# Weight sums a group later, a second tile's weights prepared in the mixer, and late value copies on ScalarE

## The chip, the cores and the metric

The kernel runs on one core of a Trainium2 chip, with float32 inputs and one output of 1024 x 1024. The metric is the time of one execution on the device in microseconds (us); of several runs the median counts. Five engines work beside each other, each on its own queue in its own order: TensorE (PE, matrix products into the eight PSUM banks), VectorE (DVE), ScalarE (ACT), GpSimd (POOL) and SyncE (SP). Transfers between the chip's memory and SBUF are issued from SP's and ACT's queues.

## The reference

A decoder block for 1024 tokens of width 1024, in float32. A state-space branch and an attention branch read one normalised input, are gated, added and projected; then come attention into 256 memory tokens and a SwiGLU feed-forward part. Cut to what matters here:

```python
def reference(x, mem, ...):
    u = rms_norm(h, norm_mix[l])
    proj = u @ w_in[l]
    u_ssm, q, k, v, f_logit, gate_logits = jnp.split(proj, [...], axis=-1)
    y_ssm = jax.nn.gelu(s5_ssm(u_ssm, ...))
    glu_a, glu_b = jnp.split(y_ssm @ w_glu[l], 2, axis=-1)
    out_a = glu_a * jax.nn.sigmoid(glu_b)
    att = forgetting_attention(q, k, v, f_logit + b_forget[l])
    out_b = att @ w_fox_o[l]
    gate_a, gate_b = jnp.split(jax.nn.sigmoid(gate_logits), 2, axis=-1)
    h = h + (gate_a * out_a + gate_b * out_b) @ w_mix_out[l]
    h = h + memory_cross_attention(rms_norm(h, norm_mem_q[l]), ...)
    f_a, f_b = jnp.split(rms_norm(h, norm_ffn[l]) @ w_ffn_in[l], 2, axis=-1)
    h = h + (jax.nn.silu(f_a) * f_b) @ w_ffn_out[l]
    return rms_norm(h, norm_final)
```

## The kernel before, in words

**Products.** PE multiplies in a reduced format; each float32 operand is split into a high and a low part, and a product is three matmuls (high by high, high by low, low by high), lines L167 to L169 and L617. The split is the helper `split`: a cast on ACT (L177) and a subtraction on DVE (L178). Weights come through `wload`: a load on SP into `raw` (two buffers, L153), then a split into `whi` and `wlo` (four buffers each). The large products with w_mix_out and the feed-forward weights go by seven products of half size in place of eight; these need sums and differences of blocks of both operands.

**Stages.** stage_in normalises and projects. stage_ssm runs 32 gate products (`gates`, 16 row blocks by two halves) and puts the four groups q of the state space between them (`todo`): `turn_weights` builds the tile Ts and shifts it by three small transfers (L1442), `toeplitz` copies it to Tt on ACT (L1447), `states` loads xg (L1453) and runs the scan, `out` multiplies by Tt (L1503). Beside them go the sums of w_mix_out's blocks that the mixer wants later (`jobs`): `mix_fetch` loads two tiles wk on SP (L491), `mix_sums` does four additions on DVE (L500), `mix_store` stores the four results to sums_d on SP (L504); wk has two buffers. Then comes the attention, and behind it stage_tail.

**The gate loop of stage_tail.** It runs over j from 0 to 7, eight row blocks of 128 channels. For j above 3 `glu.values(j)` loads weights and multiplies; `Glu.value` copies each of the two products (128 x 512) from PSUM to the tile sg, on DVE, at L1186. `glu.rest(j)` multiplies for the sigmoid (ACT, L1191), multiplies sg by it on DVE (L1192), and by the gate ga on POOL (L1199, loads at L1198). Three steps behind, `fox_part(j - 3)` multiplies the attention's output, loads gb (L545), multiplies it by the product in PSUM (L577), adds it to sg (L578), splits (A11, S3 for j below 4; A12, A22, S1, S2 above) and stores to am_d (L585) or s3_d (L593); `minuend` loads am_d back as xm (L563). PSUM banks are shared out as mm 3, sc 2, pv 2, misc 1, so that a product waits until the copy or multiplication of an earlier one has emptied its bank.

**Weights ahead.** The first two of the feed-forward part's weight tiles are prepared early. `ahead(j)` gives five steps: `fetch` loads two tiles wpr of 512 KB on SP (L642); `plain`, `sums`, `seventh` and `rest` split and add (L655 to L660 on DVE) and store seven tiles of 512 KB to w_d from ACT's queue (L633). The feed-forward stage reads w_d back much later.

**The mixer.** For the products n = 1, 2, 6, 5, 3, 7, 4 `mix_weights(n)` loads and splits weights (n = 1, 2, 3 from w_mix_out, the others from sums_d), `mix_mm(n, i)` runs four strips i of twelve matmuls, `mix_add` adds them to the tiles h. After each strip of n = 2, 6, 5 one step of the list `side` runs; it holds the two steps `mix_s4`, which load s3_d and split it. After the strips of n = 3 and n = 4 `scaled` writes the normalised rows to tiles xs, which `turned` transposes on PE.

**What sets the order.** The program is written in this order, and a scheduler then places the instructions of each engine, keeping dependences. `tc.issue_after(ins)` keeps the instructions inside it from being placed ahead of `ins` on ins's own engine. Tiles come from pools: `slot` takes one of 16 buffers, `tmp` one of 5 (shared with sg, xs and others), and a new tile in a buffer waits for the last use of the old one.

Of the kernel before, what the change touches and what calls it, by code (L numbers as in the profile page):

```python
# [9 lines left out]
F32 = mybir.dt.float32  # L10
F32R = mybir.dt.float32r
# [55 lines left out]
def f32(ap):  # L67
    return ap.bitcast(F32)
# [223 lines left out]
def hybrid_block_kernel(ctx: ExitStack, tc: tile.TileContext, x, mem, norm_mix, w_in, b_forget,  # L292
# [36 lines left out]
    with tc.tile_pool(name="st2", bufs=1, reuse_waits="tile") as s2:  # L329
        stage_tail(B, big, s2, sh, x, glu, aT, gate_d, kv_d, sums_d, w_fox_o, w_mix_out, norm_mem_q[0], w_mem_q,  # L330
                   w_mem_o, norm_ffn[0], w_ffn_in, w_ffn_out, norm_final, out)
# [124 lines left out]
def stage_ssm(B, s5, qp, uT, w_in, gate_d, u_d, y_d, w_mix_out, sums_d):  # L456
# [48 lines left out]

    jobs = {}
    for k in range(4):
        for i, f in ((7 * k + 2, mix_fetch), (7 * k + 3, mix_sums), (7 * k + 4, mix_store)):
            jobs[i] = lambda f=f, k=k: f(k)

    mark = []
# [18 lines left out]
def stage_tail(B, big, s2, sh, x, glu, aT, gate_d, kv_d, sums_d, w_fox_o, w_mix_out, g_mq, w_mem_q, w_mem_o, g_ffn,  # L530
# [7 lines left out]
    def slot(dt=F32, name="t"):  # L538
        return s2.tile([P, D], dt, tag="t", bufs=NS2, name=name)

    tmp = sh.tmp
# [16 lines left out]
    def give(name, mk, k, src):  # L558
        B.split(*[a[k // 2][:, k % 2, :] for a in operand(name, mk)], src)

    def minuend(j):
        xm[j] = s2.tile([P, D], F32, tag=("gbc", "xs")[j % 2], bufs=1, name="xm")
        S.dma_start(xm[j], am_d[j - 4])  # L563
# [63 lines left out]
    w_d = B.dram.tile([AHEAD_IN, 7, P, D], F32, name="w_d")  # L627
    pre = {}

    def ahead(j):  # L630

        def keep(n, t_):
            A.dma_start(w_d[j, n], f32(t_))  # L633

        def pair(n):
            hl = slot(F32R, "wph"), slot(F32R, "wpl")
            return hl, [[t_[:, o:o + 512] for t_ in hl] for o in (0, 512)]

        def fetch():
            pre[j] = [slot(name="wpr") for _ in range(2)]  # L640
            for r_, c in zip(pre[j], (0, FH)):
                S.dma_start(r_.rearrange("p (k c) -> p k c", k=8),  # L642
                            w_ffn_in[:, c + j * P:c + (j + 1) * P].rearrange("(k p) c -> p k c", p=P))

        def plain():
            hl, _ = pair(0)
            B.split(*hl, pre[j][0])
            for i, t_ in enumerate(hl):
                keep(i, t_)

        def sums():
            ra, rb = pre[j]
            b22 = rb[:, 512:]
            hl, (w5, w6) = pair(2)
            V.tensor_add(ra[:, 512:], ra[:, 512:], b22)  # L655
            V.tensor_add(ra[:, :512], ra[:, :512], rb[:, :512])
            V.tensor_add(rb[:, :512], rb[:, :512], b22)
            B.split(*w5, ra[:, :512])
            V.tensor_add(ra[:, 512:], ra[:, 512:], ra[:, :512])
            V.tensor_add(ra[:, :512], ra[:, :512], b22)  # L660
            B.split(*w6, ra[:, :512])
            for i, t_ in enumerate(hl):
                keep(2 + i, t_)

        def seventh():
            e_ = slot(F32R, "wph")
            B.split(e_[:, :512], e_[:, 512:], pre[j][1][:, :512])
            keep(4, e_)

        def rest():  # L670
            ra, rb = pre.pop(j)
            hl, (w3, w4) = pair(5)
            B.split(*w3, rb[:, 512:])
            B.split(*w4, ra[:, 512:])
            for i, t_ in enumerate(hl):
                keep(5 + i, t_)

        return [fetch, plain, sums, seventh, rest]

    ahead0, ahead1 = ahead(0), ahead(1)  # L680
    for j in range(8):
        if j > 3:
            for f in glu.values(j):
                f()
        glu.rest(j)
        with B.tc.issue_after(glu.mark.ins):
            for f in {0: ahead0[:1], 1: ahead0[1:2], 2: ahead0[2:3], 3: ahead0[3:] + ahead1[:1], 4: ahead1[1:2],
                      5: ahead1[2:3], 6: ahead1[3:]}.get(j, []):
                f()
        if j == 6:  # L690
            minuend(4)
            minuend(5)
        if j > 2:
            fox_part(j - 3)
# [30 lines left out]
    def mix_s4(kk):  # L725
        y = s2.tile([P, D], F32, tag=("xs", "gbc")[kk], bufs=1, name="s4")
        S.dma_start(y, s3_d[kk])
        for k in range(2):
            give("S4", slot, 2 * kk + k, y[:, 512 * k:512 * k + 512])

    side = [lambda kk=kk: mix_s4(kk) for kk in range(2)]
    mix_weights(6)
    for i in range(4):
        mix_add(1, i)
# [166 lines left out]
    def w_fetch(j):  # L901
        raws[j] = B.wpool.tile([P, RAW], F32, tag="raw", bufs=2, name="raw")[:, :D], tmp("rawb")
        for r_, c in zip(raws[j], (0, FH)):
            f = S.dma_start(r_.rearrange("p (k c) -> p k c", k=8),
                            w_ffn_in[:, c + j * P:c + (j + 1) * P].rearrange("(k p) c -> p k c", p=P))
        return f
# [156 lines left out]
    for j in range(2, NF):  # L1063
# [7 lines left out]
        f = w_fetch(j + 2) if j + 2 < NF else f  # L1071
# [91 lines left out]
class Glu:  # L1163
# [19 lines left out]

    def value(self, j, h):
        ps, dst = self.product(j, h, 0)
        self.B.V.tensor_copy(dst, ps)  # L1186

    def sigmoid(self, j, h):
        ps, dst = self.product(j, h, 1)
# [20 lines left out]
class S5:  # L1210
# [146 lines left out]
    def slot(self, name, bufs=1):  # L1357
        return self.qp.tile([P, D], F32, tag=name, bufs=bufs, name=name)
# [551 lines left out]
```

## Time and profile before

| | |
|---|---|
| median of 3 runs | 1607.4 us (1603.07 to 1611.19) |
| profiled execution, its own time | 1597.43 us |
| its span | 1595.6 us |
| mean granted clock of PE | 0.984 |
| instructions | 20523 |
| moved by transfers | 258.69 MB, mean 162 GB/s |

The profile is one execution, recorded by the hardware. A row of the timeline gives start and length in us, engine, line, operation, output and inputs, and in brackets the idle time of the engine just before and what ended it. A row of the waits gives engine and line, what it waited for, the total in us, how many times, and the longest. A row of the windows gives for a stretch of time the length, then the busy time of PE, its weight loads, DVE, ACT and POOL with the number of instructions, then PE's granted clock, the busy share of the transfer engines and GB/s. A row of the chain gives start, length, engine, tile and line.

### The profile page before, as it was taken

To read this page: it belongs to the slowest core of one execution; us is meant where nothing else is said; L and a number is where in the kernel's file an instruction comes from. 1 tells how busy PE (TensorE), PEld (TensorE's weight loads), DVE (VectorE), ACT (ScalarE), POOL (GpSimd) and SP (SyncE) were. 2 spreads that over 40 slices of the span, in tenths; PEclk is the share of its full clock that TensorE was granted. 3 is DMA by queue.
4 is the path that set the end of the run, shared out by engine and by line. 5 is a ranking of instruction groups with operands and counts; after the bars stand their busy time and mean duration, and the time that the engine had idled before them with its cause. 6 is when DMAs were issued, how large, how long until landed. Compare 5 with 4: busy or idle time off the path is not lost.

```text
span 1595.6 us, 20523 instructions
## 1 busy us (share of the span) xinstructions
PE 1527.3 (96%) x7301; PEld 1257.5 (79%) x7301; DVE 1067.9 (67%) x1900; ACT 669.6 (42%) x1191; POOL 247.9 (16%) x323
## 2 busy tenths in 40 slices
PE   5799899999999899999999989999999999999997
PEld 5688788898777668778788778888888888788886
DVE  5757666435687776888665687777677776565455
ACT  5422343422566553333345564333333333344342
POOL 3015434110121123320101200010000000000001
PEclk8999999999999999999999999999999999999999
DMA  8747745552032635977322177445444544796642
GB/s 272 143 95 170 232 122 113 126 177 31 1 68 44 163 101 180 318 244 259 120 89 84 53 272 251 156 159 165 165 152 153 164 161 147 269 389 221 193 156 106
DMA packets 202869, 258.69 MB, mean 162 GB/s; under 512 B 36024, under 2 KB 127064, under 8 KB 202256
## 3 DMA queue, kind: packets, MB, share of 16 engines
q1 hardware_dynamic: 196144, 241.67, 50.5%
q10 hardware_dynamic: 6624, 15.73, 2.6%
q8 instruction: 57, 0.93, 0.2%
q14 instruction: 44, 0.36, 0.1%
HBM read 176.08 MB, written 83.20 MB: 162 GB/s over the span
## 4 chain that ended last, share of the span: by engine, by line
PE 75%; DVE 8%; DMA 8%; issue 3%; ACT 3%; POOL 2%; SPq 1%; DVEq 0%; POOLq 0%; ACTq 0%
PE mm L967 14%; PE pv L967 7%; PE mm L167 6%; PE mm L169 6%; PE mm L168 6%; PE mm L1104 4%; PE sc L967 4%; PE sc L1104 3%; PE pv L1104 3%; PE sc L167 2%; PE sc L169 2%; PE sc L168 2%; PE mm L617 2%; PE misc L1104 1%; DMA Ts<-Ts 1%
## 5 line engine op out<-in xcount | busy, mean ns | idle before, releaser
L178 DVE TENSOR_TENSOR wlo<-raw,whi 128x1024 fp32r<-128x1024 f32 (+2 forms) x126 | 133.4, 1061 | 114.0 <-ACT whi L177 113.4
L177 ACT CAST whi<-raw 128x1024 fp32r<-128x1024 f32 (+2 forms) x127 | 115.6, 913 | 133.8 <-PE mm L168 38.0
L167 PE MATMUL mm<-uh,whi 128*128 128x512 f32 x344 | 138.2, 402 | 2.4 <-ACT whi L177 2.3
L178 DVE TENSOR_TENSOR ol<-or,oh 128x1024 fp32r<-128x1024 f32 x73 | 89.3, 1224 | 70.8 <-ACT oh L177 69.7
L169 PE MATMUL mm<-uh,wlo 128*128 128x512 f32 x344 | 135.7, 395 | 0.0
L168 PE MATMUL mm<-ul,whi 128*128 128x512 f32 x344 | 135.4, 394 | 0.0
L177 ACT CAST oh<-or 128x1024 fp32r<-128x1024 f32 x73 | 76.8, 1052 | 103.7 <-PE mm L1104 35.3
L999 POOL TENSOR_TENSOR g<-a,c 128x512 f32<-128x512 f32 x22 | 35.6, 1619 | 394.7 <-ACT a L998 374.8
L196 POOL TENSOR_TENSOR r<-ms,mhalf 128x1 f32<-128x1 f32 (+1 forms) x30 | 19.9, 666 | 372.9 <-DVE ms L192 345.3
L1729 POOL TENSOR_TENSOR pl<-pf,ph 128x512 fp32r<-128x512 f32 (+1 forms) x32 | 39.5, 1235 | 244.0 <-DVE ph L1728 198.4
L167 PEld LDWEIGHTS mm<-uh,whi 128*128 128x128 f32 x344 | 65.5, 190 | 14.7 <-ACT whi L177 2.7
L169 PEld LDWEIGHTS mm<-uh,wlo 128*128 128x128 f32 x344 | 65.3, 190 | 14.7 <-DVE wlo L178 1.3
L168 PEld LDWEIGHTS mm<-ul,whi 128*128 128x128 f32 x344 | 65.4, 190 | 11.0
L1726 ACT ACTIVATE pf<-sc 128x512 f32<-128x512 f32 (+1 forms) x96 | 46.4, 490 | 49.1 <-DVE sc L1722 29.4
L967 PE MATMUL pv<-S3h,we 128*128 128x512 f32 x176 | 58.1, 389 | 0.0
L1199 POOL TENSOR_TENSOR sg<-sg,ga 128x512 f32<-128x512 f32 x16 | 36.8, 2318 | 72.6 <-DVE sg L1192 50.8
L167 PE MATMUL mm<-yh,whi 128*128 128x512 f32 x104 | 41.8, 402 | 2.4 <-DVE sg L1186 2.4
L1732 DVE TENSOR_TENSOR pl<-pf,ph 128x512 fp32r<-128x512 f32 (+2 forms) x64 | 35.6, 558 | 10.1 <-ACT ph L1731 9.4
L169 PE MATMUL mm<-yh,wlo 128*128 128x512 f32 x104 | 41.6, 400 | 0.0
L168 PE MATMUL mm<-yl,whi 128*128 128x512 f32 x104 | 41.4, 398 | 0.0
L1104 PE MATMUL mm<-oh 128*128 128x512 f32 x106 | 41.2, 389 | 0.0
L1104 PE MATMUL mm<-ol,oh 128*128 128x512 f32 x106 | 41.2, 389 | 0.0
(680 smaller groups left out, 4581.8 us busy)
## 6 DMA issues: line engine op xcount, KB each, us to landing
or<-c_d SPq DMA_DIRECT2D x77, 256.0 KB
wo<-in_w_ffn_out_dram SPq DMA_DIRECT2D x22, 512.0 KB
c_d<-g SPq DMA_DIRECT2D x44, 256.0 KB
t_d<-wo SPq DMA_DIRECT2D x44, 256.0 KB
or<-t_d SPq DMA_DIRECT2D x44, 256.0 KB
raw<-in_w_ffn_in_dram SPq DMA_DIRECT2D x20, 512.0 KB
rawb<-in_w_ffn_in_dram SPq DMA_DIRECT2D x20, 512.0 KB
raw<-in_w_in_dram SPq DMA_DIRECT2D x18, 512.0 KB
```

The lines of the kernel that those rows point to most:

```text
L167: T.matmul(ps, lh, rh, start=first, stop=False)
L168: T.matmul(ps, lh, rl, start=False, stop=False)
L169: T.matmul(ps, ll, rh, start=False, stop=last)
L177: self.A.copy(hi, src)
L178: (self.G if pool_lo else self.V).tensor_sub(lo, src, f32(hi))
L967: T.matmul(ps, l_[:, k, :], r_, start=first and k == 0 and i == 0, stop=k == 3 and i == 2, skip_group_check=True)
L999: G.tensor_mul(g[:, 512:], a1, c1)
L1104: T.matmul(ps, l_[:, gi], r_[:, 512:], start=n < 3 and p == 0 and k == 0 or n == 7 and p == 0 and k == 0, stop=p == NP - 1 and k == 2, ski ...
L1199: self.B.G.tensor_mul(self.out[j][:, cs], self.out[j][:, cs], ga)
L1726: self.exp = A.activation(pf[:, off:], ps[:, off:], AF.Exp)
L1729: G.tensor_sub(pl[:, off:], pf[:, off:], f32(ph[:, off:]))
L1732: V.tensor_sub(pl[:, off:], pf[:, off:], f32(ph[:, off:]))
```

## The change

Three parts. The jobs on w_mix_out's sums get the places 9 to 11, 16 to 18, 23 to 25 and 29 to 31 in the list of gate products; they had 2 to 4, 9 to 11, 16 to 18 and 23 to 25. The five steps of `ahead(1)` leave the gate loop (they stood at j = 3 to 6) and join `side`, between the strips of the mixer's products, with tiles from `tmp`; `ahead(0)` now has one step at each j from 0 to 4. And `Glu.value` copies on ACT for j above 3.

```diff
@@ -505,7 +505,7 @@
 
     jobs = {}
     for k in range(4):
-        for i, f in ((7 * k + 2, mix_fetch), (7 * k + 3, mix_sums), (7 * k + 4, mix_store)):
+        for i, f in enumerate((mix_fetch, mix_sums, mix_store), (9, 16, 23, 29)[k]):
             jobs[i] = lambda f=f, k=k: f(k)
 
     mark = []
...
@@ -627,17 +627,17 @@
     w_d = B.dram.tile([AHEAD_IN, 7, P, D], F32, name="w_d")
     pre = {}
 
-    def ahead(j):
+    def ahead(j, mk):
 
         def keep(n, t_):
             A.dma_start(w_d[j, n], f32(t_))
 
         def pair(n):
-            hl = slot(F32R, "wph"), slot(F32R, "wpl")
+            hl = mk("wph", F32R), mk("wpl", F32R)
             return hl, [[t_[:, o:o + 512] for t_ in hl] for o in (0, 512)]
 
         def fetch():
-            pre[j] = [slot(name="wpr") for _ in range(2)]
+            pre[j] = [mk("wpr") for _ in range(2)]
             for r_, c in zip(pre[j], (0, FH)):
                 S.dma_start(r_.rearrange("p (k c) -> p k c", k=8),
                             w_ffn_in[:, c + j * P:c + (j + 1) * P].rearrange("(k p) c -> p k c", p=P))
...
@@ -663,7 +663,7 @@
                 keep(2 + i, t_)
 
         def seventh():
-            e_ = slot(F32R, "wph")
+            e_ = mk("wph", F32R)
             B.split(e_[:, :512], e_[:, 512:], pre[j][1][:, :512])
             keep(4, e_)
...
@@ -677,16 +677,15 @@
 
         return [fetch, plain, sums, seventh, rest]
 
-    ahead0, ahead1 = ahead(0), ahead(1)
+    ahead0, ahead1 = ahead(0, lambda name, dt=F32: slot(dt, name)), ahead(1, tmp)
     for j in range(8):
         if j > 3:
             for f in glu.values(j):
                 f()
         glu.rest(j)
         with B.tc.issue_after(glu.mark.ins):
-            for f in {0: ahead0[:1], 1: ahead0[1:2], 2: ahead0[2:3], 3: ahead0[3:] + ahead1[:1], 4: ahead1[1:2],
-                      5: ahead1[2:3], 6: ahead1[3:]}.get(j, []):
-                f()
+            if j < 5:
+                ahead0[j]()
         if j == 6:
             minuend(4)
             minuend(5)
...
@@ -728,7 +727,8 @@
         for k in range(2):
             give("S4", slot, 2 * kk + k, y[:, 512 * k:512 * k + 512])
 
-    side = [lambda kk=kk: mix_s4(kk) for kk in range(2)]
+    side = [ahead1[0]] + [lambda kk=kk: mix_s4(kk) for kk in range(2)] + ahead1[1:2] + [lambda: None] + ahead1[2:3] + \
+        [lambda: None] + ahead1[3:]
     mix_weights(6)
     for i in range(4):
         mix_add(1, i)
...
@@ -1183,7 +1183,10 @@
 
     def value(self, j, h):
         ps, dst = self.product(j, h, 0)
-        self.B.V.tensor_copy(dst, ps)
+        if j < 4:
+            self.B.V.tensor_copy(dst, ps)
+        else:
+            self.B.A.copy(dst, ps)
 
     def sigmoid(self, j, h):
         ps, dst = self.product(j, h, 1)
```

In the changed kernel the lines from L1187 on are three lower in the file: L1191, L1192 and L1198 are L1194, L1195 and L1201, L1442 and L1453 are L1445 and L1456; the copy on ACT is L1189.

**Sums of the state groups, on SP.** Before, SP's queue where the first group's xg load (L1453) stands; wk are the tiles of the sums, raw the gate products' weights:

```order
L491 DMA wk_1317<-in_w_mix_out_dram 128x1024
L491 DMA wk_1318<-in_w_mix_out_dram 128x1024
L1453 DMA xg_1425<-u_d_77 128x1024
L504 DMA sums_d_84<-wk_1317 128x512 x2
L504 DMA sums_d_84<-wk_1318 128x512
L491 DMA wk_1757<-in_w_mix_out_dram 128x1024
L504 DMA sums_d_84<-wk_1318 128x512
L504 DMA sums_d_84<-wk_1757 128x512
L491 DMA wk_1758<-in_w_mix_out_dram 128x1024
L153 DMA raw_1659<-in_w_in_dram 128x4x256
```

The change, at the same place:

```order
L1456 DMA xg_1413<-u_d_77 128x1024
L491 DMA wk_1745<-in_w_mix_out_dram 128x1024
L491 DMA wk_1746<-in_w_mix_out_dram 128x1024
L504 DMA sums_d_84<-wk_1745 128x512 x2
L504 DMA sums_d_84<-wk_1746 128x512 x2
L491 DMA wk_2185<-in_w_mix_out_dram 128x1024
L491 DMA wk_2186<-in_w_mix_out_dram 128x1024
L153 DMA raw_1647<-in_w_in_dram 128x4x256
L504 DMA sums_d_84<-wk_2185 128x512
L153 DMA raw_1653<-in_w_in_dram 128x4x256
```

xg has moved ahead of the first two wk, the four stores of the first group stand together, and both wk of the second group stand ahead of the two raw loads.

**The value copies.** Before, DVE's queue from the second tile's split (wpl) to the first value copy of j = 5 (L1186, sg_6419):

```order
L178 TENSOR_TENSOR S3l_6274<-sg_5719,S3h_6272 128x512
L178 TENSOR_TENSOR wlo_6536<-raw_6532,whi_6535 128x1024
L178 TENSOR_TENSOR wpl_6354<-wpr_6221,wph_6353 128x1024
L577 TENSOR_TENSOR gb_6372<-gb_6372,pv_6359 128x512
L578 TENSOR_TENSOR sg_5802<-sg_5802,gb_6372 128x512
L577 TENSOR_TENSOR gb_6389<-gb_6389,pv_6376 128x512
L178 TENSOR_TENSOR A11l_6267<-sg_5802,A11h_6265 128x512
L578 TENSOR_TENSOR sg_5802<-sg_5802,gb_6389 128x512
L1186 COPY sg_6419<-mm_6406 128x4x128
```

The change, on ACT's queue, with the two copies of j = 5 (L1189, sg_6409); whi_6630 is the weight cast of j = 7, wph and wpl here are the first tile's:

```order
L1194 ACTIVATE sb_6332<-sc_6319 128x512
L177 CAST whi_6512<-raw_6509 128x1024
L633 DMA w_d_6033<-wpl_6342 128x1024
L177 CAST whi_6630<-raw_6627 128x1024
L1189 COPY sg_6409<-mm_6396 128x4x128
L177 CAST A11h_6253<-sg_5802 128x512
L1189 COPY sg_6409<-mm_6411 128x4x128
L177 CAST S3h_6260<-sg_5802 128x512
```

The copies have left DVE and stand on ACT behind a weight cast and a store of the first tile, one on each side of A11h.

**SP ahead of fox_part(4).** Before, SP's queue from the gb loads of fox_part(3) to those of fox_part(4), with what each row waits for:

```order
L545 DMA gb_6652<-gate_d_79 128x512 [waits DMAHW2_49,DVE_49]
L153 DMA raw_6958<-in_w_mix_out_dram 128x2x512 [waits DMAHW4_49,DVE_49]
L585 DMA am_d_6031<-sg_5972 128x1024 [waits DMAHW6_49,DVE_49]
L153 DMA raw_6964<-in_w_mix_out_dram 128x2x512 [waits DMAHW7_49,DVE_49]
L1198 DMA ga_6730<-gate_d_79 128x512 [waits DMAHW0_49,Pool_49]
L1198 DMA ga_6733<-gate_d_79 128x512 [waits DMAHW1_49]
L545 DMA gb_6755<-gate_d_79 128x512 [waits DMAHW2_49]
L545 DMA gb_6778<-gate_d_79 128x512 [waits DMAHW3_49,DVE_49]
```

The change, at the same place:

```order
L153 DMA raw_6923<-in_w_mix_out_dram 128x2x512 [waits DMAHW4_49,DVE_49]
L153 DMA raw_6929<-in_w_mix_out_dram 128x2x512 [waits DMAHW6_49,DMAHW5_49,DVE_49]
L585 DMA am_d_6031<-sg_5972 128x1024 [waits DVE_49]
L642 DMA wpr_7058<-in_w_ffn_in_dram 128x8x128 [waits DMAHW7_49,DMAHW6_49,DVE_49]
L1201 DMA ga_6695<-gate_d_79 128x512 [waits DMAHW1_49,DMAHW0_49,Pool_49]
L1201 DMA ga_6698<-gate_d_79 128x512
L545 DMA gb_6720<-gate_d_79 128x512 [waits DMAHW2_49]
L545 DMA gb_6743<-gate_d_79 128x512 [waits DMAHW3_49,DVE_49]
```

The raw load that stood behind the am_d store now stands ahead of it, and behind the store stands the first half of the second tile's fetch (wpr_7058, L642), ahead of the ga and gb loads.

## The prediction

> **What bounds the kernel now.** I read the page first, then the TensorE waits, then the rows around the waits that lie in the two stages the change touches.
>
> ```profile
> PE 1527.3 (96%) x7301; PEld 1257.5 (79%) x7301; DVE 1067.9 (67%) x1900; ACT 669.6 (42%) x1191; POOL 247.9 (16%) x323
> ```
>
> TensorE (PE) is busy 96% of the span and the change adds or removes no matmul. So it can only give or take idle time of PE, and time in which PE runs at a lower clock. The waits of PE in the two stages:
>
> ```profile
> PE pv L1503 <- ACT Tt L1447: 3.6, 1, 3.6
> PE pv L167 <- DVE gb L577: 2.8, 1, 2.8
> PE mm L167 <- DVE sg L1186: 2.4, 1, 2.4
> PE pv L1460 <- DMA xg<-u_d: 1.6, 1, 1.6
> PE misc L222 <- DVE u2l L178: 1.3, 1, 1.3
> ```
>
> The first and fourth lie in the state groups (stage_ssm, 168 and 196 us), the second and third in the gate loop of stage_tail (713 and 667 us), the fifth in the mixer (796 us). Together 11.7 us, 0.7% of the run: that is the ceiling, apart from the clock.
>
> **First stall of the tail, 667 us.** The rows of PE, then the granted clock (PEclk, third number from the right) of three windows, each behind a stall:
>
> ```profile
> 666.78 0.39 PE L168 MATMUL mm<-yl,whi 128*128 128x512 f32 x1
> 667.00 0.39 PE L169 MATMUL mm<-yh,wlo 128*128 128x512 f32 x1
> 669.84 0.50 PE L167 MATMUL mm<-yh,whi 128*128 128x512 f32 x1 [2.45 <-DVE sg L1186]
> ...
> 674.28 0.40 PE L167 MATMUL pv<-ath,whi 128*128 128x512 f32 x1
> ...
> 690.64 0.39 PE L167 MATMUL pv<-ath,whi 128*128 128x512 f32 x1
> ...
> 715.85 0.50 PE L167 MATMUL pv<-ath,whi 128*128 128x512 f32 x1 [2.84 <-DVE gb L577]
> ```
>
> ```profile
> 670.30:673.80 3.50, 3.50 (x10) 2.71 (x9) 1.36 (x3) 2.06 (x3) 0.00 (x0) 0.51 0.73 277
> 712.50:716.00 3.50, 0.66 (x4) 0.24 (x3) 1.41 (x3) 0.00 (x0) 2.16 (x2) 1.00 0.88 328
> 172.00:175.40 3.40, 3.29 (x15) 3.29 (x16) 0.00 (x0) 0.66 (x2) 2.77 (x13) 0.50 0.20 77
> ```
>
> Matmuls start 0.22 to 0.23 us apart when nothing holds them (666.78, 667.00), so the one at 669.84 is 669.84 - 667.00 - 0.23 = 2.6 us late. Behind it the clock is halved: 12 matmuls take 674.28 - 669.84 = 4.44 us in place of 12 x 0.227 = 2.7, another 1.7 us. This place costs **4.3 us**. What it waits for is a copy on VectorE (DVE), L1186:
>
> ```profile
> 662.66 1.21 DVE L178 TENSOR_TENSOR wpl<-wpr,wph 128x1024 fp32r<-128x1024 f32 x1
> ...
> 664.80 0.69 DVE L577 TENSOR_TENSOR gb<-gb,pv 128x512 f32<-128x512 f32 x1 [0.94 <-DMA gb<-gate_d]
> ...
> 668.72 1.07 DVE L1186 COPY sg<-mm 128x512 f32<-128x512 f32 x1
> ```
>
> The copy of value(5, 0) stands in program order behind the second tile's split (wpl) and a gb that waits for its load, and so its mm bank comes free at 669.8. In the changed kernel it is on ScalarE (ACT), behind one weight cast. ACT at this time is nearly empty:
>
> ```profile
> 666.85 0.62 ACT L177 CAST A11h<-sg 128x512 fp32r<-128x512 f32 x1 [6.45 <-DVE sg L578]
> ...
> 672.84 0.59 ACT L1191 ACTIVATE sb<-mm 128x512 f32<-128x512 f32 x1
> ```
>
> An ACT pass over a 128x512 PSUM bank takes 0.59 us (L1191). The bound below is nothing, the bound above 1.07 (the DVE copy); I take 0.6. The cast ahead (whi_6630) needs its raw weights: before, their load stood on SP behind a wpr fetch, am_d, ga, gb and xm; now it stands ahead of all but the gb of group 0, so some 8 us earlier. The last thing ACT waits for ahead of the copy is the first tile's wpl split on DVE, at about 660 by adding up the DVE rows between. So the copy runs at about 662.5 to 663.5, against 667.2 when PE needs it: 4 us of margin. I take the whole 4.3 as gained. If the raw load were as slow as before (it takes 8 us then) the margin is gone, and up to 2 us of stall stay.
>
> By the Trainium skill, "TensorE: Matmul & The Clock Gate", section "Why this matters for your kernels", the clock falls only after idle gaps of more than about 3 us; by it this stall would not have halved the clock, and the sum below would be 1.7 us smaller. The rows here go against it in both directions: 2.45 us of idle is followed by a clock of 0.51, 2.84 us at 713 by 1.00; the measured rows decide.
>
> **Second stall of the tail, 713 us.** The chain of work that ended last runs through SP's queue:
>
> ```profile
> 707.12 1.14 DVE wlo L178
> 708.27 0.38 SPq L153
> ...
> 709.74 5.28 DMA gb<-gate_d
> 715.11 0.70 DVE gb L577
> ```
>
> The gb of fox_part(4) is issued only at 709.74, because SP stood ahead of it at the am_d store and a raw load, both waiting for DVE; it lands 5.28 us later, frees a pv bank, and fox_part(5) starts at 715.85, 2.84 us after PE was idle, 3.0 after it could have started. DVE is late because of what the change takes off it in this stretch (640 to 720 us, by groups):
>
> ```profile
> L1186 DVE COPY sg<-mm 128x512 f32<-128x512 f32 x8 | 8.9, 1133 | 0.0
> L178 DVE TENSOR_TENSOR wpl<-wpr,wph 128x512 fp32r<-128x512 f32 (+1 forms) x10 | 7.7, 791 | 4.2 <-ACT wph L177 4.2
> ```
>
> How far it is behind, at group 3:
>
> ```profile
> 701.43 0.70 DVE L577 TENSOR_TENSOR gb<-gb,pv 128x512 f32<-128x512 f32 x1
> ```
>
> PE begins group 3 at 690.64 and has its first half 12 matmuls later, at 693.4; DVE multiplies it at 701.43, 8 us late.
>
> 8.9 us of copies go to ACT. Of the splits and sums of the two prepared tiles about half belong to the second: one 1.21 split, five of 0.7, and five sums, about 9 us. So DVE loses 18 of 80 us in this stretch and stays close behind PE; the am_d store of group 3 goes out near 696 instead of 707 (4.3 since PE is earlier, some 7 of the 8 that DVE is late).
>
> But the order shows something new on SP: the first half of the second tile's fetch (wpr, 512 KB) now stands between that store and the gb loads, and it takes the slot that the store reads, so SP stops until the store has landed. The same pair of store and dependent load once before:
>
> ```profile
> 658.82 0.34 SPq L585 DMA_DIRECT2D am_d<-sg  x1
> ...
> 662.31 0.32 SPq L563 DMA_DIRECT2D xm<-am_d  x1
> ```
>
> 3.5 us. So: store 696, fetch 699.5, ga and gb issued by 701.4, gb landed 5.3 later at 706.7. PE, 4.3 earlier than before, wants the bank at 712.85 - 4.3 = 708.5; less 0.7 for the multiply, 707.8. About 1 us of margin. I take the whole **3.0** as gained. The bounds are nothing (the wait at the store eats it) and 3.0.
>
> **State groups.** The chain there:
>
> ```profile
> 148.17 12.78 DMA Ts<-Ts
> 160.97 3.21 DMA Ts<-Ts
> 164.20 6.73 DMA Ts<-Ts
> 171.01 1.05 ACT Tt L1447
> ...
> 190.78 7.21 DMA xg<-u_d
> ```
>
> Three small shifts, 12.78 + 3.21 + 6.73 us, make the 3.6 us stall, and xg, which stands on SP behind four sums_d stores, the 1.6 us one. The change names later places for the sums, but what it adds is an edge on ACT's program, and fetch, sums and stores are on SP and DVE. In the order, the stores and sums of the first two groups stand within a few rows of where they stood, and from the third on nothing differs. What is left: the first group's xg load is ahead of the first wk fetches, four stores go out earlier, and both wk of the second group before the raw loads. These last bear on two DVE rows:
>
> ```profile
> 150.38 1.42 DVE L500 TENSOR_TENSOR wk<-wk 128x512 f32<-128x512 f32 x2 [2.50 <-DMA wk<-in_w_mix_out_dram]
> ...
> 187.94 2.14 DVE L500 TENSOR_TENSOR wk<-wk 128x512 f32<-128x512 f32 x3 [1.64 <-DMA wk<-in_w_mix_out_dram]
> ```
>
> The idle 2.50 goes and the first Ts shift may land sooner: up to 2.5 us off the stall and 1.0 off the half clock behind it (clock 0.50 above). But one more 512 KB load stands ahead of it, up to 2 us the other way, and the xg wait behind it swallows a gain. Range -3.5 to +2; I take **-1**.
>
> **Mixer.** Here the second tile's work lands: about 7.5 us of DVE (the 1.21, and ten passes at the 0.65 that its quicker rows show), 1 MB of loads and seven stores of 512 KB. DVE has room, DMA less:
>
> ```profile
> 740.00:760.00 20.00, 20.00 (x90) 16.55 (x89) 16.45 (x25) 8.46 (x14) 0.00 (x0) 1.00 0.80 300
> 760.00:780.00 20.00, 20.00 (x90) 16.58 (x89) 11.58 (x15) 5.60 (x8) 0.00 (x0) 1.00 0.50 164
> ```
>
> DVE is idle 3.55 + 8.42 = 12 us in these 40, more than 7.5. The tightest piece is the weights of the product n=5:
>
> ```profile
> 760.97 1.22 DVE L178 TENSOR_TENSOR wlo<-raw,whi 128x1024 fp32r<-128x1024 f32 x1
> ...
> 764.50 0.39 PE L617 MATMUL mm<-whi,S1h 128*128 128x512 f32 x1
> ```
>
> They are whole at 762.2 and used from 764.5, the second half from 765.9: 2.3 and more to spare. One w_d store ahead of their load is 0.5 MB at 300 GB/s, 1.7 us. I take **0** for the mixer, with bounds of -1 (the 1.3 us wait at 796, where the turns move by one to four matmuls) and +4 (two stores and the fetch ahead, 5 us, less 2.3, and half a clock window of 1.7).
>
> **Sum:** -4.3 - 3.0 - 1 + 0 = **-8.3 us**, from the profiled execution's 1597.43 us to 1589.1. That execution was 10 us quicker than the median of the runs, 1607.4; on the median the forecast is **1599**.
>
> **The rivals.**
> - *The second stall stays.* If the store lands later than 700, or the 512 KB fetch makes gb slower than 5.3 us, SP's new wait takes the place of the old one. For it: 1 us of margin and a DMA share of 0.88 there. Against it: the 4.5 MB of the second tile are otherwise gone from this stretch. -5.3 us, 1602.
> - *The mixer gives it back, and more.* The 3.5 MB of stores, 12 us at 300 GB/s, go out on ACT's queue in front of the weight loads of n=5, n=3 and n=7, and ACT's casts stand behind stores that wait for DVE. It decides once a weight load is over 2.3 us later. Each product that starts late costs 3 to 4 us and a half-clock window of 1.7; with all three late, 15 us, less 8.3: 1614, slower. For it: DMA at 0.80 already. Against it: three products have 11 us each to load. By the Trainium skill, "DMA: Bandwidth & Descriptors", section "Issuing engines are not separate DMA queues", transfers from either queue share the same engines and interleave; by that rule the stores do hold up the loads, and nothing in this trace speaks against it.
> - *The part on the state groups does what it says.* Then both waits (3.6 + 1.6) and the 1.7 of clock go: another -6, 1593. Against it: the order.
>
> **How the numbers follow.** Forecast as summed: 0.60. Second stall stays: 0.14. Mixer gives back: 0.16, two thirds of it slower than before by over 0.5%. More gain than summed: 0.10. A measurement of this kernel can tell about 0.5%, 8 us, from no change; the forecast lies on that bound, so a little over half of it counts as faster. Faster 0.33 + 0.10 + 0.02 = 0.45, same 0.45, slower 0.10. The range holds the forecast with the runs' own spread of 4 us either way, the second stall, and the near end of the mixer's rival: 1592 to 1610.
>
> **What would show it.** Right: no PE idle at 667 and a clock of 1.00 behind it; no wait on gb at L577 by 713; eight COPY rows of ACT in place of those of DVE; the sums (L500) at the same times as before. Wrong: a wait of PE on gb at 705 to 712 with SP waiting for am_d; a wait on whi or wlo at the start of n=5, n=3 or n=7; a Ts stall at 168 that is gone or doubled.

## The result, and the profile after

| | before | changed |
|---|---|---|
| median, 11 runs each | 1604.24 us (1597.42 to 1611.19) | 1596.33 us (1591.59 to 1602.31) |
| ratio of changed to before, 95% interval | | 0.995, 0.993 to 0.997 |
| the profiled execution, its own time | 1597.43 us | 1591.59 us |
| its span, mean clock | 1595.6 us, 0.984 | 1589.8 us, 0.985 |

The changed kernel is 1604.24 - 1596.33 = 7.9 us faster, half a per cent. The sum of the prediction was 8.3. The terms below did not come out as well as their sum.

The page of the changed kernel, busy time of each engine, share of the span and instructions:

```profile
PE 1526.6 (96%) x7301; PEld 1256.5 (79%) x7301; DVE 1059.3 (67%) x1892; ACT 678.2 (43%) x1199; POOL 245.8 (15%) x323
```

PE's work is the same; the eight copies went from DVE's count to ACT's. PE's waits in the tail of the changed kernel, 600 to 820 us (total, times, longest):

```profile
PE pv L167 <- DVE gb L577: 2.5, 1, 2.5
PE misc L222 <- DVE u2l L178: 1.0, 1, 1.0
PE misc L222 <- DVE h L624: 1.0, 1, 1.0
```

The wait on the copy (sg) is gone. The wait on gb, which I had counted as gone, is there. First the copies: ACT's rows around 662 us, and its group of copies from 640 to 720 us (count, busy us, mean ns, idle before):

```profile
660.89 0.33 ACTq L633 DMA_DIRECT2D w_d<-wpl  x1
661.33 1.05 ACT L177 CAST whi<-raw 128x1024 fp32r<-128x1024 f32 x1 [1.97 <-DVE wpl L178]
662.29 1.12 ACT L1189 COPY sg<-mm 128x512 f32<-128x512 f32 x1
```

```profile
L1189 ACT COPY sg<-mm 128x512 f32<-128x512 f32 x8 | 9.0, 1152 | 0.0
```

The copy of value(5, 0) ends at 663.4, 2.6 us before PE takes its bank at 666.0. (The prediction's 667 is the clock of the execution before; this one is 1.3 us ahead of it already where fox_part(0) starts, at 636.06 in place of 637.31.) A copy takes 1.15 us on ACT in the mean, about what it took on DVE (1.13), not the 0.6 of an ACTIVATE of the same size, and a little more than the 1.07 that the prediction had as its upper bound.

Now the wait that stayed. (A transfer "lands" where the profile has its end.) SP's queue in the changed kernel around it, SP's wait there, and PE's two matmuls on either side of the stall:

```profile
698.79 0.34 SPq L585 DMA_DIRECT2D am_d<-sg  x1
702.59 0.37 SPq L642 DMA_DIRECT2D wpr<-in_w_ffn_in_dram  x1
703.07 1.20 SPq L1201 DMA_DIRECT2D ga<-gate_d  x2
704.33 6.22 SPq L545 DMA_DIRECT2D gb<-gate_d  x5
```

```profile
SPq L642 <- DMA am_d<-sg: 3.4, 1, 3.4
```

```profile
707.01 0.39 PE L617 MATMUL mm<-w1l,A11h 128*128 128x512 f32 x1
709.92 0.50 PE L167 MATMUL pv<-ath,whi 128*128 128x512 f32 x1 [2.53 <-DVE gb L577]
```

SP stands from the store (698.79) to the second tile's fetch (702.59), because that fetch takes the slot that the store reads. Behind it come ga and then the gb of fox_part(4). The chain that ended last goes through the same rows:

```profile
698.07 0.70 DVE sg L583
698.79 3.73 DMA am_d<-sg
...
702.59 0.37 SPq L642
...
704.33 4.76 DMA gb<-gate_d
...
709.18 0.70 DVE gb L577
...
709.92 0.50 PE pv L167
```

So the rival called "the second stall stays" is what the trace shows: the new wait at the fetch took the place of the old ones. PE is 709.92 - 707.01 - 0.23 = 2.7 us late here, where it was 3.0 before.

DVE's groups of L577 between 640 and 712 us, the changed kernel first, then before (count, busy us, mean ns, idle just before them and its cause):

```profile
L577 DVE TENSOR_TENSOR gb<-gb,pv 128x512 f32<-128x512 f32 x10 | 6.7, 682 | 14.4 <-DMA gb<-gate_d 14.4
```

```profile
L577 DVE TENSOR_TENSOR gb<-gb,pv 128x512 f32<-128x512 f32 x8 | 5.4, 680 | 0.9 <-DMA gb<-gate_d 0.9
```

Before, DVE was late by its own work. Now it has less work, and stands 14.4 us for gb loads in the same 72 us; 9.9 of them lie ahead of the store at 698.79, the last 4.5 are the stall itself. The chain of the changed kernel ahead of that store:

```profile
655.21 2.62 DMA am_d<-sg
...
659.80 5.93 DMA gb<-gate_d
...
670.93 4.27 DMA am_d<-sg
...
676.61 5.93 DMA gb<-gate_d
...
688.81 4.22 DMA gb<-gate_d
```

So only a part of DVE's free time was turned into an earlier store: DVE waits for a load, the store waits for DVE, and the next load waits on SP behind the store.

The mixer, two windows (length, then busy us of PE, PEld, DVE, ACT and POOL, then clock, share of the transfer engines, GB/s):

```profile
740.00:760.00 20.00, 20.00 (x90) 16.57 (x89) 19.93 (x30) 7.14 (x12) 0.00 (x0) 1.00 0.83 301
760.00:780.00 20.00, 20.00 (x90) 16.58 (x89) 12.55 (x20) 8.89 (x16) 0.89 (x2) 1.00 0.70 248
```

DVE is full in the first of them and the transfers went from 0.50 to 0.70 in the second, yet PE does not stop once: the second tile's work found its room. (By the clock these are the prediction's windows; the work in them is some 6 us further on, as n=2 starts at 736.81 in place of 742.74.)

### The profile page after: what moved, and what is told of

Same layout as the page of the kernel before. It is cut to its first block, busy times and chain, and to the rows that moved or that the text cites. A ratio compares the mean times of both kernels' runs of the same rounds, so it can differ in the third digit from the quotient of the medians.

```text
span 1589.8 us, 20526 instructions
## 1 busy us (share of the span) xinstructions
PE 1526.6 (96%) x7301; PEld 1256.5 (79%) x7301; DVE 1059.3 (67%) x1892; ACT 678.2 (43%) x1199; POOL 245.8 (15%) x323
## 4 chain that ended last, share of the span: by engine, by line
PE 73%; DVE 10%; DMA 8%; issue 3%; POOL 2%; ACT 2%; SPq 1%; DVEq 0%; POOLq 0%; ACTq 0%
PE mm L967 15%; PE pv L967 7%; PE mm L167 6%; PE mm L168 6%; PE mm L169 6%; PE mm L1104 5%; PE sc L967 4%; PE sc L1104 4%; PE pv L1104 3%; PE sc L167 2%; PE sc L169 2%; PE sc L168 2%; PE misc L1104 2%; DMA gb<-gate_d 1%; DVE wlo L178 1%
## 5 line engine op out<-in xcount | busy, mean ns | idle before, releaser
L178 DVE TENSOR_TENSOR wlo<-raw,whi 128x1024 fp32r<-128x1024 f32 (+2 forms) x126 | 133.8, 1063 | 109.0 <-ACT whi L177 108.6
L167 PE MATMUL mm<-uh,whi 128*128 128x512 f32 x344 | 139.0, 404 | 2.1 <-ACT whi L177 2.0
L178 DVE TENSOR_TENSOR ol<-or,oh 128x1024 fp32r<-128x1024 f32 x73 | 89.3, 1223 | 70.5 <-ACT oh L177 69.3
L167 PEld LDWEIGHTS mm<-uh,whi 128*128 128x128 f32 x344 | 65.9, 192 | 14.5 <-ACT whi L177 2.4
L1202 POOL TENSOR_TENSOR sg<-sg,ga 128x512 f32<-128x512 f32 x16 | 33.7, 2125 | 70.9 <-DVE sg L1195 30.0
L1104 PE MATMUL mm<-oh,ol 128*128 128x512 f32 x106 | 41.2, 389 | 0.0
L167 PE MATMUL mm<-yh,whi 128*128 128x512 f32 x104 | 40.9, 393 | 0.0
L167 PE MATMUL sc<-uh,whi 128*128 128x512 f32 x104 | 40.8, 393 | 0.0
```

What stands on the lines that cost most here:

```text
L167: T.matmul(ps, lh, rh, start=first, stop=False)
L178: (self.G if pool_lo else self.V).tensor_sub(lo, src, f32(hi))
L1104: T.matmul(ps, l_[:, gi], r_[:, 512:], start=n < 3 and p == 0 and k == 0 or n == 7 and p == 0 and k == 0, stop=p == NP - 1 and k == 2, ski ...
L1202: self.B.G.tensor_mul(self.out[j][:, cs], self.out[j][:, cs], ga)
```

## The experiments

Several kernels were run in each of three groups; the kernel before was run in each group on the same chip, and a ratio is always against those runs. To see where the time goes I also cut each trace at two rows of PE: the first matmul of fox_part(0) (L167, pv) and the first of the product n=2 (L617, sc<-whi,A12h). Between them lies the gate loop, counted from fox_part(0). From there to the first matmul of the memory attention lies the rest of the mixer.

**One part at a time.** e1_sums is the kernel before with only the later places of the sums:

```diff
-        for i, f in ((7 * k + 2, mix_fetch), (7 * k + 3, mix_sums), (7 * k + 4, mix_store)):
+        for i, f in enumerate((mix_fetch, mix_sums, mix_store), (9, 16, 23, 29)[k]):
```

> The kernel before with only the jobs of the weight sums at their new places. Theory (the order hardly moves, since the edge is on ACT's program and the jobs are on SP and DVE): about -1 us against the kernel before, between -3 and +1; the Ts wait near 168 us shrinks by 1 to 2 us and the xg wait near 195 us grows by about 1. Rival (the sums do come a group later and both waits of the state groups go): -5 us, no wait of PE on Tt or xg left. The stalls at 667 and 713 us stay in both.

Measured: 1603.56 us against 1603.98, ratio 1.0002 (0.9986 to 1.0018). No change that these runs can tell: the interval goes from 2.2 us less to 2.9 us more. PE's waits of e1_sums in the state groups:

```profile
PE pv L1460 <- DMA xg<-u_d: 3.8, 1, 3.8
...
PE pv L1503 <- ACT Tt L1447: 2.2, 1, 2.2
```

The wait for Tt is shorter than before (2.2, it was 3.6), the wait for xg behind it longer (3.8, it was 1.6): 6.0 us together in place of 5.2. Over all 14 traces it is the same, in the mean: with the new places of the sums (seven traces) the wait for Tt is 2.1 us and that for xg 2.6, with the old ones (seven) 2.7 and 1.9. With the wait for the tile m from ACT (L1429 of before) the three sum to 5.3 and 5.2.

e1_copies is the kernel before with only the copies on ACT:

```diff
-        self.B.V.tensor_copy(dst, ps)
+        if j < 4:
+            self.B.V.tensor_copy(dst, ps)
+        else:
+            self.B.A.copy(dst, ps)
```

> The kernel before with only the value copies from j = 4 on ScalarE. Theory (the copies alone don't free the queue: in this order the copy of value(5, 0) stands on ACT behind the A11h cast, which waits for DVE and its gb load): the stall at 667 us shrinks from 2.6 to 1 to 1.5 us, the stall at 713 by some 1 to 3 us as DVE has 9 us less to do and no fetch is in SP's way: -2 to -5 us in all. Rival (the copies are the whole gain): -7 to -8 us. Second rival (copies do nothing without the second part): within 1 us of the kernel before.

Measured: 1603.79 us, ratio 0.9987 (0.9972 to 1.0002): by the ratio about 2 us, by the medians 0.2, and not certain. Two of PE's waits in its trace:

```profile
PE pv L167 <- DVE gb L577: 6.5, 2, 4.9
...
PE mm L167 <- ACT sg L1189: 0.3, 1, 0.3
```

The wait on the copy is down to 0.3, and the time is lost again at the gb: 6.5 us in two waits, in place of 2.8 in one. The expectation had this second stall shrink; it grew.

e1_tile is the kernel before with only the second tile's steps in the mixer:

```diff
-    ahead0, ahead1 = ahead(0), ahead(1)
+    ahead0, ahead1 = ahead(0, lambda name, dt=F32: slot(dt, name)), ahead(1, tmp)
...
-    side = [lambda kk=kk: mix_s4(kk) for kk in range(2)]
+    side = [ahead1[0]] + [lambda kk=kk: mix_s4(kk) for kk in range(2)] + ahead1[1:2] + [lambda: None] + ahead1[2:3] + \
+        [lambda: None] + ahead1[3:]
```

> The kernel before with only the second feed-forward tile moved to the mixer. Theory (its work on DVE and its transfers make the first stall; its fetch on SP keeps the second): no stall or under 1 us at 667 and a full clock behind it, the wait on gb of fox_part(4) stays at 2 us or more behind SP's wait for the am_d store, the mixer costs about 1 us: -3 to -5 us. Rival (copies on DVE keep the first stall): -1 us or slower.

Measured: 1601.37 us, ratio 0.9983 (0.9972 to 0.9995), some 2.7 us, just short of the 3 to 5 expected. And the wait is not where it was expected. Here it is the other way round: no wait on gb, and a longer one on the copy. The chain of e1_tile that leads to it:

```profile
658.63 0.70 DVE sg L583
...
659.35 2.61 DMA am_d<-sg
...
661.98 0.33 SPq L563
...
663.71 6.21 DMA gb<-gate_d
...
670.01 0.09 DVE gb L577
...
673.03 0.99 DVE sg L1186
...
674.07 0.50 PE mm L167
```

PE's matmul at 674.07 came 674.07 - 669.00 - 0.23 = 4.8 us late, though the second tile's split is no longer ahead of the copy on DVE. What holds the copy is the gb in front of it in DVE's order, and that gb is late by the same pattern: store, its landing, a load that waits for it (xm, L563), and the gb behind that load on SP. Taking work off DVE does not help this copy; taking it out from behind the gb does: in none of the traces with the copies on ACT does PE wait more than 0.3 us for one.

**Both parts of the tail, without the sums.** e2_no_sums is the changed kernel with the old places of the sums (the reverse of the first diff). e2_before and e2_after are the two kernels once more, one execution each with its trace.

> The changed kernel with the jobs of the weight sums at their old places: the second and third part together. Theory (the first part is worth nothing, the other two free the gate loop only together): the time of the changed kernel, -7 to -8 us against the kernel before, the wait on gb of fox_part(4) near 707 us still there at 2 us or more, none at 667. Rival (the first part is worth the rest): -4 us, the sum of the second and third part alone (-2 and -3).

> The kernel before once more, for a second trace. Question: whether the trace shown is typical of the tail, or whether its two stalls (2.6 and 3.0 us) differ from one execution to the next. If the stages ahead of the tail vary by several us (the first product of fox_part(0) began between 636 and 643 us in six traces) and the tail by less than 1, then the tail of the kernel before is again 176 to 177 us from there to the first product of the memory attention. If the stalls vary, it is 178 or more, and the shown execution was a quick one.

> The changed kernel once more, for a second trace. The same question: 172 to 173 us from the first product of fox_part(0) to the first product of the memory attention if the tail is steady; the wait on gb near 707 us again between 2 and 3 us, behind SP's wait for the am_d store of 3 to 4 us.

Measured: e2_no_sums 1594.5 us against 1600.89, ratio 0.996 (0.9945 to 0.9975); e2_before 1599.85, e2_after 1595.85 in their single executions. The two tail parts alone give 6.4 us, an interval that overlaps that of the whole change. Apart they gave about 2 and 2.7; in its trace each alone hands much of its time from one wait to the other. That the two are worth more together than their sum is not shown: 6.4 and 4.7 us lie too close for these intervals.

**The new wait at the fetch taken away.** e1_late_fetch is the changed kernel with the second tile's fetch held on SP until the last gb load has been issued (its lines stand two, later six, further down in the file):

```diff
+    loads = []
...
-        S.dma_start(t_, src)
+        loads.append(S.dma_start(t_, src))
...
-    side = [ahead1[0]] + [lambda kk=kk: mix_s4(kk) for kk in range(2)] + ahead1[1:2] + [lambda: None] + ahead1[2:3] + \
+    def fetch_late():
+        with B.tc.issue_after(loads[-1].ins):
+            ahead1[0]()
+
+    side = [fetch_late] + [lambda kk=kk: mix_s4(kk) for kk in range(2)] + ahead1[1:2] + [lambda: None] + ahead1[2:3] + \
```

> The changed kernel with the second tile's fetch held on SP behind the last gb load. Theory (SP's wait for the am_d store ahead of the fetch, 3.4 us, is what keeps the second stall of 2.5 to 2.7 us): no wait of PE on gb near 707 us, gb of fox_part(4) issued about 4 us earlier after the store, 2.5 us less than the changed kernel, so -10 us against the kernel before. Rival (SP's order of store before gb load is late by itself): the wait stays above 1.5 us and the time is that of the changed kernel. If the later fetch then delays the mixer, a wait of PE on weights appears at the start of n = 6, 5 or 3.

Measured: 1592.17 us, ratio 0.993 (0.9909 to 0.9951). Its SP queue at the place, and PE's wait on gb:

```profile
701.23 0.34 SPq L587 DMA_DIRECT2D am_d<-sg  x1
701.69 1.15 SPq L1207 DMA_DIRECT2D ga<-gate_d  x2
702.88 7.23 SPq L547 DMA_DIRECT2D gb<-gate_d  x5
...
718.51 0.43 SPq L644 DMA_DIRECT2D wpr<-in_w_ffn_in_dram  x1
```

```profile
PE pv L167 <- DVE gb L579: 0.2, 1, 0.2
```

The store is here 2.4 us later by the clock than in the changed kernel, and gb is still issued 1.45 us earlier, because nothing between them waits for the store. Counted from the start of fox_part(0), the store stands where it stood (62.8 us, in the changed kernel 62.7), and gb goes out 3.8 us earlier. PE waits 0.2 us for gb here, and in the three other traces with the late fetch its matmul is at most 0.2 us late at this place. This shows that the second stall of the changed kernel is the wait at the fetch.

The gate loop says the same in every trace (us, from the rows named above; gb issue is counted from the first matmul of fox_part(4), the gap is between the starts of the two matmuls around the second stall, 0.23 without a stall):

| trace | gate loop | rest of mixer | gb issued | gap |
|---|---|---|---|---|
| before | 105.4 | 71.2 | +2.8 | 3.2 |
| e2_before | 105.3 | 71.2 | +4.0 | 4.4 |
| e1_sums | 107.2 | 71.2 | +3.9 | 4.7 |
| e1_copies | 107.6 | 71.2 | +5.9 | 5.3 |
| e1_tile | 104.5 | 70.1 | -1.5 | 0.2 |
| e3_store_act | 104.3 | 70.7 | +3.2 | 3.6 |
| changed | 100.7 | 71.6 | +3.0 | 2.9 |
| e2_after | 104.9 | 70.2 | +5.4 | 5.6 |
| e3_after | 103.9 | 70.2 | +4.6 | 4.4 |
| e2_no_sums | 102.1 | 70.9 | +1.6 | 2.9 |
| e1_late_fetch | 98.4 | 70.7 | -0.8 | 0.6 |
| e2_late_no_sums | 98.3 | 72.4 | +0.4 | 0.4 |
| e3_late | 97.9 | 72.4 | -1.1 | 0.2 |
| e3_late_store_act | 97.9 | 71.8 | -0.6 | 0.2 |

(The late fetch without the sums and the e3 runs are described below.) A gb that is issued before fox_part(4) begins, or 0.4 us behind, costs next to nothing; one that is issued 1.6 us or more behind costs 2.6 us and more. In the changed kernel the fetch went out 3.8 us behind the store in one trace and 5.5 and 5.2 in e2_after and e3_after, and the gap follows it.

**The late fetch without the sums.** e2_late_no_sums is e1_late_fetch with the old places of the sums.

> The changed kernel with the second tile's fetch held behind the last gb load and the jobs of the sums at their old places. Theory (first part worth nothing): -11 us against the kernel before, as with the late fetch alone, no wait of PE on gb or sg in the gate loop. Rival (the first part gains 1 to 3 us once the tail is clean): -8 to -10.

Measured: 1592.1 us against 1600.89, ratio 0.9947 (0.9929 to 0.9965), gate loop 98.3. As far as these runs can tell, the late fetch does not need the sums either.

**The store on another queue.** e3_store_act is the kernel before with the am_d store issued from ACT's queue, so that SP never waits for it; e3_late_store_act is the late fetch with the same:

```diff
-            S.dma_start(am_d[j], sg)
+            A.dma_start(am_d[j], sg)
```

> The kernel before with one line changed: the am_d store of fox_part is issued from ACT's queue, behind the S3h cast that waits for the same DVE result anyway, in place of SP's, so that the ga and gb loads behind it no longer wait for DVE. Theory (SP's wait for DVE at the am_d store ahead of the next gb loads makes the waits on gb): the wait on gb near 713 us falls from 3 to 4 us to under 1, 3 to 4 us less than the kernel before; the wait at 667 us, a full DVE and a copy, stays or shrinks by a microsecond. Rival (DVE is late by itself, with the second tile and the copies on it): both waits stay, within 1 us of the kernel before.

> The changed kernel with the fetch held behind the last gb load and the am_d store on ACT's queue: both ways to clear SP. Theory: with the late fetch no wait on gb is left, so the store's move adds nothing: the same time as with the late fetch alone, -9 to -11 us against the kernel before. Rival (there is still slack to win in the loop): 1 to 2 us less than the late fetch. Second rival (the ACT order, with the copy of value(5, 0) behind A11h, brings the wait at 667 us back): 1 to 3 us more.

Measured: 1599.58 us against 1603.01, ratio 0.9977 (0.9961 to 0.9994), and 1593.45, ratio 0.9942 (0.9926 to 0.9958). SP's queue of e3_store_act:

```profile
700.42 6.31 SPq L153 DMA_DIRECT2D raw<-in_w_mix_out_dram  x2
706.84 1.14 SPq L1198 DMA_DIRECT2D ga<-gate_d  x2
708.04 6.88 SPq L545 DMA_DIRECT2D gb<-gate_d  x5
```

Without the store SP stops all the same, at the raw loads, which wait for DVE to free their buffers; gb goes out at 708.04, 3.2 us behind the start of fox_part(4), and PE's wait on gb is 3.2. So in the kernel before the store was not alone in holding gb, and moving it leaves the second stall in this trace about as it was; where the 0.23% come from is not shown (the first stall is only 1.1 us in this trace, but it was 1.6 in one of the unchanged kernel). With the late fetch it adds nothing that can be told (0.9942 beside 0.9931 below).

**Changed kernel and late fetch side by side.** e3_after is the changed kernel, e3_late is e1_late_fetch, on the same chip.

> The changed kernel on the same chip as the two versions with a late fetch, to compare them head to head: -6 to -8 us against the kernel before, the wait on gb near 707 us of 2.5 to 5 us.

> The changed kernel with the fetch held behind the last gb load, on the same chip as the changed kernel. Theory: 2.5 to 4 us less than the changed kernel, the size of its wait on gb; no wait on gb over 0.5 us. Rival (what the first run showed was the chip): the same as the changed kernel within 1 us.

Measured: 1594.44 us, ratio 0.994 (0.9926 to 0.9954), and 1593.04, ratio 0.9931 (0.9917 to 0.9946). The late fetch beats the kernel before clearly; against the changed kernel its lead of 1.4 us can't be told from nothing. That is less than the 2.5 to 4 expected. In the traces its gate loop is 103.9 - 97.9 = 6.0 us shorter and its mixer 72.4 - 70.2 = 2.2 us longer, with a wait of PE in e3_late that e3_after does not have:

```profile
PE misc L222 <- DVE h L626: 1.5, 1, 1.5
```

Over all traces the rest of the mixer takes 71.8 us in the mean of the four with the late fetch and 70.7 in the four with the changed tail. So it seems that the late fetch, which pushes the second tile's work on DVE further into the mixer, gives a part of the gain back there. That is not shown: e1_late_fetch has no such wait, and the first trace of the changed kernel has one of 1.0 us.

## Why the prediction came out as it did

**First stall (-4.3): right in kind, too large in size.** It is gone from every trace with the copies on ACT (PE waits 0.3 us at most), the copy started at 662.29 where I had put it at 662.5 to 663.5, and in the changed kernel no half clock followed. But I sized it by one execution. In the three traces with the unchanged loop (before, e2_before, e1_sums) the matmul was 2.6, 1.6 and 2.2 us late, and only the first lost 1.7 to the clock behind it: 2.7 in the mean. And of the two things that I named ahead of the copy on DVE, the split of the second tile was not the one that mattered. e1_tile took it away and the stall grew; the gb that waits for its load held the copy.

Of the three windows with which the prediction shows the clock, the second (712.50 to 716.00) lies inside its stall and not behind it. Behind it, from 716 to 722, the clock is 1.00 too, so the reading stands. But a full clock after 2.84 us of idle time agrees with the bound of about 3 us that the prediction cites from the Trainium skill; only the half clock after 2.45 us goes against it, and not both rows as I wrote.

**Second stall (-3.0): wrong.** It stayed, at 2.7 us in the profiled execution and 5.4 and 4.2 in e2_after and e3_after. The step that failed is "the am_d store of group 3 goes out near 696", and under it "DVE is late because of what the change takes off it". The store went out at 698.79. DVE did get freer. The window from 640 to 712 us of before, then of the changed kernel (length, then the busy time of PE, PEld and DVE):

```profile
640.00:712.00 72.00, 69.55 (x300) 57.05 (x299) 64.22 (x76) 24.66 (x38) 23.34 (x10) 0.98 0.82 280
```

```profile
640.00:712.00 72.00, 69.47 (x307) 57.23 (x306) 51.42 (x60) 28.88 (x39) 20.73 (x12) 1.00 0.71 240
```

Its busy time fell by 12.8 us, some 5 less than the 18 I had counted for a slightly longer stretch. But it then stood 14.4 us for gb loads, 9.9 of them ahead of the store, because the loop of store, landing and next load on SP runs at its own pace. DVE did not come "close behind PE": the gb of group 3 was issued only at 688.81, behind the store of group 2 (687.15), and DVE multiplied it at 693.13, 5.4 us behind PE's product (685.0 and twelve matmuls, 687.7), where it had been 8 late before and I had counted about 1.

I had worked out the new wait of SP at the fetch and its 3.5 us rightly (it was 3.8), and then given the store ahead of it too much credit, more than the 1 us of margin. By the clock that is 2.8 us; but this execution was 1.3 us ahead from fox_part(0) on. Counted from there, the store came forward from 69.8 to 62.7 us, by 7.1 and not by the 11.2 of the prediction, 4.0 us too much; PE wanted the bank at 707.01 + 0.23 = 707.2, which is 71.2 us behind the start of fox_part(0), just as forecast. The rival had this mechanism with a chance of 0.14, and its condition (a store that lands later than 700) was met: 702.5. Its time, 1602 us, was not.

**State groups (-1): nothing that can be told.** The part alone has the ratio 1.0002, and -1 us lies inside its interval. The swap that I named is what the traces show: the wait for xg takes what the wait for Tt loses. Naming it, I should have put the term at 0. The sums stay about where they were, as the order had said: the last of the rows L500 starts at 187.94 before and at 187.60 in the changed kernel.

**Mixer (0): right.** From n=2 to the memory attention it takes 71.2 us in the old traces and 70.2 to 71.6 in the changed kernel's. The rival that had the mixer give everything back needed a weight load over 2.3 us late; no product waited.

**The sum (-8.3): right, and as far as the traces go by luck.** Measured 7.9, and in the later runs beside e3_late 8.6. The terms as the traces bear them out are 2.7 for the first stall and about nothing for the second. The gate loop of the unchanged traces takes 106.0 us in the mean of three, that of the changed tail (with e2_no_sums) 102.9 in the mean of four. That is 3.1 us, and 0.5 come from the mixer. Some 4 us of the measured gain are not found in these stretches.

The spans of the seven traces tell a little more. They differ by 6.5 us in the mean (1599.1 and 1592.6). 3.1 are the gate loop, 0.5 the rest of the mixer, and 0.2 lie from the memory attention to the end (781.9 and 781.7). The other 2.7 lie ahead of fox_part(0), which starts at 640.0 and 637.3 in the mean, but anywhere from 635.5 to 642.6 in all 14 traces. The one part that works there is the sums, and alone they gave nothing that could be told, so scatter between executions is the likely cause; it is not shown. Single executions of one kernel differ by 11 to 14 us, and each trace is one of them: the first gate product of the tail (L167, mm<-yh) alone starts anywhere between 575.2 and 580.7 us, and from there to fox_part(0) an execution of either kind takes 60.3 or 61.6 to 61.9 us (the last section says why). Whether the untraced executions lose more in the old loop than the traced ones stays open, and so does the cause of these 4 us, half of the gain.

What a loop without either stall gives is shown by e1_late_fetch: 98.4 us, against 105.4 in the trace of before. That is 7.0, beside the 7.3 which I had summed for the two stalls from that trace. The prices were about right for that execution; the changed kernel just does not remove the second.

## What to carry to other kernels

When an engine is late, look at whether it is late by its work or by a loop through a queue: here a store waits for DVE, a load behind it on SP's queue waits for the store to land, and DVE waits for that load, so taking 13 us of work off DVE in good part made it wait. Before a load is moved on an in-order queue, look at what its buffer was used for last: a load that reuses the buffer of a store just issued stops everything behind it for the whole landing (3.8 us here), and here the cure was to place it behind the loads that are needed first. Size a stall from several executions where there are any; one trace had it at 4.3 us where the mean was 2.7.

## What the runs showed of the hardware

**The same gap halves the clock in one execution and not in another.** Every trace has, at 581 to 589 us, a gap of 2.0 us between the starts of two of PE's matmuls, where a product of the attention waits for POOL. The matmul behind it and the window that follows, in the changed kernel first and then in e2_late_no_sums:

```profile
583.57 0.44 PE L1754 MATMUL pv<-pl,vhi 128*65 128x512 f32 x1 [1.68 <-POOL pl L1732]
```

```profile
583.50:587.00 3.50, 3.44 (x18) 2.55 (x18) 2.50 (x6) 1.25 (x4) 0.01 (x1) 1.00 0.39 132
```

```profile
587.45 0.69 PE L1760 MATMUL pv<-pl,vhi 128*65 128x512 f32 x1 [1.69 <-POOL pl L1738]
```

```profile
587.40:590.80 3.40, 3.35 (x9) 2.44 (x10) 1.96 (x4) 0.98 (x3) 0.00 (x0) 0.51 0.35 121
```

Granted clock 1.00 and 18 matmuls in the one, 0.51 and 9 in the other. From the first gate product to fox_part(0) the 14 traces take either 60.3 to 60.4 us (8 of them) or 61.6 to 61.9 (6): the half clock costs 1.3 us here, and it is not the kernel that decides: before and e2_before are the same kernel and differ in it (61.6 and 60.4), and so do e1_late_fetch and e3_late (60.3 and 61.7). In the gate loop too, a gap of 2.9 us halved the clock in e2_no_sums (0.56 in the 3.5 us behind it) and not in the changed kernel (1.00). By the Trainium skill, "TensorE: Matmul & The Clock Gate", section "What's actually happening", the window in which activity is watched runs freely and is not reset when a kernel starts. A dependence on where the gap falls would fit these rows, though no run here shows the window itself. The bound of about 3 us that the prediction takes from the Trainium skill, section "Why this matters for your kernels" of the same title, does not hold here: 2.0 us of gap were enough in 6 of 14.

**Some passes of DVE are slowed beside a multiplication of POOL.** In e1_copies, a pass of DVE of 128x512 alone, two of them beside POOL, and POOL's row:

```profile
698.21 0.68 DVE L178 TENSOR_TENSOR wph<-wpr,wph 128x512 fp32r<-128x512 f32 x1
698.81 3.48 DVE L178 TENSOR_TENSOR wpl<-wpr,wph 128x512 fp32r<-128x512 f32 x2
```

```profile
698.39 3.36 POOL L1202 TENSOR_TENSOR sg<-sg,ga 128x512 f32<-128x512 f32 x2 [14.85 <-DVE sg L1195]
```

The two passes take 3.48 us in place of some 1.3, and POOL's two multiplications cover nearly all of that time. It is not every pass. From 600 to 760 us of the 14 traces DVE has 494 such passes (L178, 128x512). The 424 with no multiplication of POOL beside them take 0.67 to 0.74 us. Of the 70 others 14 take over 1 us, up to 1.80, while 44 that lie wholly inside a multiplication take 0.72 at most. What decides between them no run here shows. So the mean of a group can hide passes of two and a half times its shortest.
